# The first branch's projection in pairs of time blocks, and the end of a hybrid RWKV-7 / S5 block in two passes over weights kept in SBUF

## The chip, the core and the metric

The kernel runs on one core of one Trainium2 chip. The metric is the time of one execution on the device in microseconds (us), lower is better. TensorE is called PE here, its weight loads PEld, VectorE DVE, ScalarE ACT, GpSimd POOL, and SyncE, which only issues transfers, SP.

## The reference

One block of a streaming encoder over 2048 frames (T) of width 1024 (D), all in float32. An RMSNorm is followed by one input projection, whose columns feed two branches and three kinds of gates. The RWKV-7 branch has 16 heads of 64, the S5 branch 32 groups of 16 channels (width 512). Both are recurrences in time.

```python
h = rms_norm(x, norm_g)
zs, gate_a, u, gate_b, m_a, m_b = jnp.split(h @ w_in, SPLIT_POINTS, axis=-1)
...
y_a = y.reshape(bsz, seq, RWKV_WIDTH) * jax.nn.silu(gate_a)     # y: the RWKV-7 recurrence over zs
ys = jax.nn.gelu(s5_scan(u, ...))                               # 512 channels
g1, g2 = jnp.split(ys @ w_glu + b_glu, 2, axis=-1)
y_b = g1 * jax.nn.sigmoid(g2) * jax.nn.silu(gate_b)
merged = jax.nn.sigmoid(m_a) * (y_a @ p_a) + jax.nn.sigmoid(m_b) * (y_b @ p_b)
out = rms_norm(x + merged @ w_out, final_g)
```

w_in is 1024 x 7296, w_glu 512 x 1024, p_a and w_out 1024 x 1024, p_b 512 x 1024.

## The kernel before

**Products.** An f32 operand is split in a high part that PE takes as f32r (a copy on ACT) and the rest (a subtraction on DVE); helpers split and split_w do this. Each product is then three matmuls for every 128 rows of the contraction: high by high, high by low, low by high. Time is cut in four blocks (NTB) of 512 columns (TB). A product of 128 output channels by 512 columns is collected in one PSUM bank; over 1024 rows it has 24 matmuls, over 512 rows 12. A piece of weights is 512 x 128 (256 KB), held as 128 partitions x 512.

**The stream of jobs.** A Job (L471) is one column block of 128 weights of a large projection with one or two time blocks: it loads the weights in two pieces, splits them, and runs 24 matmuls for each time block, in steps of 6. `stream` (L519) runs the jobs one after another as a generator, and the sequential parts of the program (the RWKV scan, later the S5 loop) call it for a step whenever they have credit. So the order on PE is set by the program: a chain of small dependent matmuls, and between its links steps of 6 matmuls of jobs. A job whose `need` is not true yet makes `stream` yield without a matmul. `late` and `rest_` hold instructions that are put a step later on their engine. DVE is used through a wrapper (Woven, L75), so most of DVE's rows bear line 75, and the tiles tell them apart.

**The scan.** `scan` (L939) goes over units of a head pair and a time block, the last ones (7,2) and (7,3). In each chunk of 64 frames PE computes px, DVE copies it to rh, PE computes pu, DVE and ACT write SU, PE computes pn, and DVE writes the next chunk's SU. The branch's output y_a goes to DRAM (ya_d).

**The first branch's projection.** `stage_a` (L650) makes a job for one column block m of p_a and one time block (tiles raw_pa, whi_pa, wlo_pa, bank ppa); its end multiplies the gate sg and stores the product to pa_d. There are 32 such jobs, time block 0 first, m from 0 to 7 in each, so each weight is loaded and split four times. Their input comes from `load_ya` (L629), a background of other jobs that is called at each step of theirs: eight times it loads 128 rows into one of two tiles (tag xh) and splits the piece before it, in 19 steps in all, into yhi and ylo, of which there are two sets. The load of block 0 runs behind the last jobs of the projection before (pmb), that of block 1 behind the jobs of block 0, and so on. A job needs the whole block and all units of the scan before its own columns to be stored.

**The S5 loop.** `s5_run` (L1209) prepares tables (tables_e makes cw with DVE and ACT; `spread` copies cw to both halves of ce by two DMAs on SP, L1260; tables_m makes kps, mps and tps on PE) and then goes over 32 groups: head (px = input times a table on PE), middle (DVE: xx from px and ce, a running sum pp, yy), tail (py on PE), and a gelu for every second group. The steps of jobs that are left are spread over its 160 steps by a rate, (LEFT - KEEP) / 160, where LEFT is the number of steps left in the stream.

**The end** (L1609 to L1690) is outside of the section that is ordered by hand; there the scheduler of the tile framework orders the instructions by their dependences. For each time block: load ys and split it; for m in 0 to 3 load and split a weight of g2, 12 matmuls into one of two banks (pg), tanh on ACT, one DVE operation with gate_b (g2th), the same for g1, and split the result (ybhi, yblo); then for m in 0 to 7 load and split a weight of p_b, 12 matmuls (ppb), DVE operations with the gate (sgb) and the first branch's product (pal), and split the sum (mhi, mlo); then for four rows of 128 frames two products of 24 matmuls with w_out (pout, two banks of their own), the residual, the norm and a store on SP's queue. w_out is loaded and split once, in time block 0, and kept (wohi, wolo). The weights of the GLU and of p_b are loaded and split in each of the four time blocks.

## Time and profile before

| what | value |
|---|---|
| three runs | 2684.04 to 2690.86 us, median 2689.07 |
| the profiled execution's own time | 2685.18 us |
| its span in the trace | 2683.5 us |
| mean clock granted to PE | 0.991 of full speed |
| DRAM traffic | 220.43 MB read, 71.70 MB written |
| instructions | 48845 |

The profile is one execution. An engine's busy time says how long its instructions lasted, as the profiler has them; for PE the ends of matmuls are modelled, so the number of matmuls in a stretch is the better measure. Windows are given in us from the start of the span, and every window has the clock that PE was granted in it. A row of the timeline has start, length, engine, line, operation, tiles, and in brackets the idle time before it with what ended it. Where rows belong to groups, they have busy time and mean duration in ns, and then the idle time before. Buffer numbers are left out of names there.

The stretches of this execution that the change touches: the jobs of p_a begin in the last units of the scan, shortly after 1956 us; the first px of the S5 loop stands at 2125; the first product of the GLU begins at 2288; the last matmul ends at 2676.

### The profile page before, as it was taken

Reading aid. Unit: us, or ns where it says so; the run is one execution under the profiler, and the core shown is the slowest. Engines: PE = TensorE matmul, PEld = TensorE weight load, DVE = VectorE, ACT = ScalarE, POOL = GpSimd, SP = SyncE. Lnnn points to the kernel's source line nnn. Section 1 sums busy time; section 2 is a strip of 40 time slices with the busy share of each in tenths; the row PEclk is TensorE's granted clock in tenths of the full one; section 3 lists DMA queues with packets and bytes.
Section 4 is the critical chain, followed back from the end, with each engine's and each line's share of the span. In section 5 each row is a group of like instructions: output and inputs, shape, how many; then the busy total and the mean of one; then the engine's idle time right before and its main releaser. Section 6 shows DMA issues by size and latency. Waiting matters only on the chain. (4 is left out here: it accounts for less than half of the span.)

```text
span 2683.5 us, 48845 instructions
## 1 busy us (share of the span) xinstructions
PE 2594.4 (97%) x17164; PEld 1970.1 (73%) x17164; DVE 1865.4 (70%) x5572; ACT 1397.7 (52%) x3501; POOL 571.9 (21%) x955
## 2 busy tenths in 40 slices
PE   7999999999999999999999999999989899899998
PEld 5777777777777767777777777777767678677787
DVE  6656677776667778767776677776768798645644
ACT  5456555655555677555555555555644443423321
POOL 2221212122122333221212122121322201111110
PEclk9999999999999999999999999999999999999999
DMA  4232323233233543332323333232565755845532
GB/s 129 77 84 67 104 74 100 76 86 87 79 97 84 146 121 104 91 86 72 97 72 93 90 85 88 73 99 73 148 180 177 216 156 161 259 155 172 170 108 95
DMA packets 256491, 304.04 MB, mean 113 GB/s; under 512 B 159761, under 2 KB 172150, under 8 KB 255222
## 3 DMA queue, kind: packets, MB, share of 16 engines
q1 hardware_dynamic: 210646, 151.46, 21.0%
q0 software_dynamic: 45600, 149.46, 18.6%
q8 instruction: 135, 2.21, 0.3%
q14 instruction: 110, 0.90, 0.1%
HBM read 220.43 MB, written 71.70 MB: 109 GB/s over the span
## 5 line engine op out<-in xcount | busy, mean ns | idle before, releaser
L962 ACT ACTIVATE SU<-pu,dd 64x64 f32<-64x64 f32 x256 | 79.3, 310 | 350.5 <-DVE SU L75 286.5
L886 DVE TENSOR_TENSOR TM<-RF,IX 128x60 f32<-128x60 f32 (+24 forms) x992 | 207.2, 209 | 29.5 <-DMA IX<-ld 7.5
L890 DVE TENSOR_TENSOR RF<-RF,TM 128x60 f32<-128x60 f32 (+24 forms) x992 | 206.8, 208 | 27.4
L953 ACT ACTIVATE us<-SU,dec 64x64 f32<-64x64 f32 x512 | 176.4, 345 | 50.1 <-DVE SU L974 43.2
L75 DVE TENSOR_SCALAR SU<-pu,dd 64x64 f32<-64x64 f32 x256 | 69.8, 273 | 137.7 <-PE pu L960 60.7
L75 DVE TENSOR_TENSOR AT<-A,amask 64x256 f32<-64x256 f32 (+1 forms) x256 | 102.2, 419 | 63.1 <-PE A L835 41.9
L974 DVE SCALAR_TENSOR_TENSOR SU<-pn,dec,us 64x64 f32<-64x64 f32 x240 | 65.6, 273 | 115.1 <-PE pn L966 113.9
L840 ACT ACTIVATE AT<-A,dd 64x64 f32<-64x64 f32 x512 | 116.9, 303 | 48.2 <-PE A L835 43.1
L966 PEld LDWEIGHTS pn<-SU,BT 128*64 128x64 f32 x1024 | 56.3, 135 | 103.7 <-issue 39.4
L957 PEld LDWEIGHTS po<-AR,SU 64*64 64x64 f32 x1024 | 50.0, 131 | 97.3 <-issue 82.8
L75 DVE COPY rh<-px 128x128 f32<-128x128 f32 x256 | 74.0, 289 | 61.8 <-PE px L948 57.2
L948 PEld LDWEIGHTS px<-SU,AT 128*128 128x128 f32 x512 | 95.1, 189 | 29.7 <-DVE SU L75 9.0
L501 PE MATMUL ppa<-yhi,whi_pa 128*128 128x512 f32 x256 | 115.3, 450 | 0.3 <-DVE sg L75 0.3
L501 PE MATMUL pmb<-hhi,whi_mb 128*128 128x512 f32 x256 | 111.7, 436 | 0.0
L501 PE MATMUL pma<-hhi,whi_ma 128*128 128x512 f32 x256 | 111.1, 434 | 0.0
L501 PE MATMUL pga<-hhi,whi_ga 128*128 128x512 f32 x256 | 110.9, 433 | 0.0
L501 PE MATMUL pr<-hhi,whi_r 128*128 128x512 f32 x256 | 110.8, 433 | 0.0
L501 PE MATMUL pk<-hhi,whi_k 128*128 128x512 f32 x256 | 110.3, 431 | 0.0
L501 PE MATMUL pv<-hhi,whi_v 128*128 128x512 f32 x256 | 109.8, 429 | 0.3 <-ACT carry L454 0.3
L503 PE MATMUL ppa<-yhi,wlo_pa 128*128 128x512 f32 x256 | 103.8, 406 | 3.6 <-DVE wlo_pa L75 3.6
L948 PE MATMUL px<-SU,AT 128*128 128x128 f32 x512 | 100.0, 277 | 4.5 <-DVE SU L75 4.3
L502 PE MATMUL ppa<-ylo,whi_pa 128*128 128x512 f32 x256 | 103.5, 404 | 0.4 <-DVE ylo L75 0.4
(376 smaller groups left out, 7926.7 us busy)
## 6 DMA issues: line engine op xcount, KB each, us to landing
IX<-ld SPq DMA_DIRECT2D x128, 128.0 KB
raw_pa<-in_p_a_dram POOLq DMA_DIRECT2D x64, 256.0 KB, 4.3
raw_mb<-in_w_in_dram POOLq DMA_DIRECT2D x50, 256.0 KB, 3.6
raw_r<-in_w_in_dram POOLq DMA_DIRECT2D x36, 256.0 KB, 4.0
raw_k<-in_w_in_dram POOLq DMA_DIRECT2D x36, 256.0 KB, 3.9
raw_v<-in_w_in_dram POOLq DMA_DIRECT2D x36, 256.0 KB, 3.4
raw_ga<-in_w_in_dram POOLq DMA_DIRECT2D x34, 256.0 KB, 3.5
ce<-cw SPq DMA_DIRECT2D x16, 514.0 KB
```

The costliest lines, as they stand in the source:

```text
L75: r = f(*a, **kw)
L501: pe.matmul(ps, hi[:, k, :], xhi[:, kk_, :], start=(kk_ == 0), stop=False)
L502: pe.matmul(ps, hi[:, k, :], xlo[:, kk_, :], start=False, stop=False)
L503: pe.matmul(ps, lo[:, k, :], xhi[:, kk_, :], start=False, stop=(kk_ == 7))
L840: act.activation(out=at[HS[h], c, 0, h, :], in_=pas[h][HS[h], i, 0:C], func=AF.Copy, scale=dd[HS[h], c:c + 1])
L886: raw_dve.tensor_tensor(out=tm[:, 0:na, 0:nt], in0=rf[:, 0:na, s:s + 1].to_broadcast([P, na, nt]), in1=ix[:, s:s + 1, s + 1:32].to_broadca ...
L890: raw_dve.tensor_tensor(out=rf[:, 0:na, s + 1:32], in0=rf[:, 0:na, s + 1:32], in1=tm[:, 0:na, 0:nt], op=ALU.add)
L948: pe.matmul(px[:, 0:P], at[:, c, 0].rearrange("p h t -> p (h t)"), cur, start=True, stop=True)
L953: act.activation(out=us[HS[h]], in_=cur[HS[h], HS[h]], func=AF.Copy, scale=dec[HS[h]])
L962: act.activation(out=cur[64:128, 64:128], in_=pu[64:128, 0:C], func=AF.Copy, scale=dd[64:128, c:c + 1])
L966: pe.matmul(pn[HS[h], 0:C], bt[:, c, h, :], cur[:, HS[h]], start=True, stop=True)
L974: (raw_dve if h == 0 else dve).scalar_tensor_tensor(out=nxt, in0=pn[HS[h], 0:C], scalar=dec[HS[h]], in1=us[HS[h]], op0=ALU.mult, op1=ALU.add)
```

## The change

**The first branch's projection.** The column blocks 0 to 2 keep one job for each time block, the blocks 3 to 7 get jobs of two time blocks, (0, 1) and (2, 3), so that one weight tile serves 1024 columns. The order is now: 0 to 2 of block 0, 3 to 7 of blocks 0 and 1, 0 to 2 of block 1, 0 to 2 of block 2, 3 to 7 of blocks 2 and 3, 0 to 2 of block 3. So 44 pieces of p_a are loaded and split instead of 64. `load_ya` loads its eight pieces straight into ylo, four at a step, and splits them there in place: 11 steps instead of 19. The gate tiles come from one pool, and KEEP goes from 1 to 4. The loads of ys for the first time block wait until at most 12 steps of jobs are left.

**The end** is now ordered by hand and has two passes. Pass 1 does the GLU of all four time blocks, in 32 products of 12 matmuls that go round five PSUM banks, and stores y_b to DRAM (yb_d). With each product one piece of weights is fetched and one split: the last four of the GLU, eight of p_b and sixteen halves of w_out, and all stay in SBUF. Pass 2 goes over the four time blocks with p_b, the merge, w_out and the norm; y_b comes back from DRAM into yblo and is split in place. What closes a product is recorded behind the next product. The stores of the output go to POOL's queue, but for the last.

Loads of GLU weights go from 32 to 8, of p_b's from 32 to 8, of w_out from 8 of 512 KB to 16 of 256 KB, of gate_b from 4 of 1 MB to 16 of 256 KB; 16 stores and 16 loads of y_b come new. PE has 12750 instructions before and after, DVE 5574 and 5514, ACT 3439 and 3379.

The diff, cut:

```diff
-KEEP = 1
-SG0 = 4
-SG1 = 24
+KEEP = 4
-ALT = 2
...
+    yb_d = [dtile(f"yb_d{i}", [512, TB]) for i in range(NTB)]
...
-            raws = []
-            for k in range(9):
-                while k < 8 and (k, tb) not in YA:
+            for k in range(8):
+                while (k, tb) not in YA:
                     yield
-                if k < 8:
-                    raws.append(gp.tile([P, TB], F32, tag="xh", name=f"yraw{tb}_{k}"))
-                    pool.dma_start(out=raws[k], in_=ya_d[tb][k * P:(k + 1) * P, :])
+                pool.dma_start(out=hlo[:, k, :].bitcast(F32), in_=ya_d[tb][k * P:(k + 1) * P, :])
+                if k % 4 == 3:
                     yield
-                if k == 8:
-                    yield
-                    yield
-                    yield
-                if k:
-                    split_later(hhi[:, k - 1, :], hlo[:, k - 1, :], raws[k - 1])
-                    yield
+            yield
+            for k in range(8):
+                hi, lo = hhi[:, k, :], hlo[:, k, :]
+                act.copy(hi, lo.bitcast(F32))
+                rest_.append(lambda hi=hi, lo=lo: dve.tensor_tensor(out=lo, in0=lo.bitcast(F32), in1=hi.bitcast(F32), op=ALU.subtract))
+                yield
             YL.add(tb)
...
-                    pl, tag = (hp, "xw") if m % 2 and SG0 <= 8 * tb + m < SG1 else (gp, "sq")
+                    pl, tag = gp, "sq"
...
-            j.pre, j.alt, j.early = pre, 8 * tbs[0] + m >= ALT, SG0 <= 8 * tbs[0] + m < SG1
+            j.pre, j.alt, j.early = pre, (m, tbs) not in ((0, (0,)), (1, (0,))), False
...
-                    if j >= YJ and step in (0, 4):
+                    if j >= YJ and LEFT[0] <= 4 * len(one_) and step in (0, 4):
...
-        jobs += with_bg([stage_a(m, (0,)) for m in range(8)], load_ya(1), 1, False)
-        late_jobs = [stage_a(m, (1,)) for m in range(8)]
-        jobs += with_bg(late_jobs, load_ya(2), 1, False)
-        jobs += with_bg([stage_a(m, (2,)) for m in range(8)], load_ya(3), 1, False)
-        jobs += [stage_a(m, (3,)) for m in range(8)]
+        one_, two_ = range(3), range(3, 8)
+        jobs += with_bg([stage_a(m, (0,)) for m in one_], load_ya(1), 1, False)
+        jobs += [stage_a(m, (0, 1)) for m in two_]
+        jobs += with_bg([stage_a(m, (1,)) for m in one_], load_ya(2), 1, False)
+        jobs += with_bg([stage_a(m, (2,)) for m in one_], load_ya(3), 1, False)
+        jobs += [stage_a(m, (2, 3)) for m in two_]
+        jobs += [stage_a(m, (3,)) for m in one_]
...
+            banks = [psg, psg, psm, psm, psm]
+            turn_ = [0]
+
+            def bank(name):
+                pl = banks[turn_[0] % 5]
+                turn_[0] += 1
+                return pl.tile([P, TB], F32, tag="g" if pl is psg else "m", name=name)
...
+            def fetch():
+                w = next(wl, None)
+                if w:
+                    ST["n"] = ST.get("n", -1) + 1
+                    flying.append((load_4(w[0], w[1], (e0, wp)[ST["n"] % 2], "raw"), w[2]))
+
+            def split_next():
+                if flying:
+                    raw, dst = flying.pop(0)
+                    split_later(*dst, raw)
...
+            def close_glu(tb, m, h, ps):
+                if h == 2:
+                    th = ST["th", m] = e0.tile([P, TB], F32, tag="gth", name=f"g2th{m}_{tb}")
+                    act.activation(out=th, in_=ps, func=AF.Tanh, bias=col(57 + 4, m, pd), scale=0.5)
+                    dve.scalar_tensor_tensor(out=th, in0=th, scalar=1.0, in1=ST.pop(("gb", tb, m)), op0=ALU.add, op1=ALU.mult)
+                else:
+                    th = ST.pop(("th", m))
+                    dve.scalar_tensor_tensor(out=th, in0=ps, scalar=col(85, m), in1=th, op0=ALU.add, op1=ALU.mult)
+                    sp.dma_start(out=yb_d[tb][m * P:(m + 1) * P, :], in_=th)
+
+            def yb_load(tb):
+                YB[tb] = [wo.tile([P, 4, TB], F32R, tag="yb" + t_, name=f"yb{t_}{tb}") for t_ in ("hi", "lo")]
+                for k in range(4):
+                    sp.dma_start(out=YB[tb][1][:, k, :].bitcast(F32), in_=yb_d[tb][k * P:(k + 1) * P, :])
+
+            def yb_split(tb, k):
+                hi, lo = (t_[:, k, :] for t_ in YB[tb])
+                halves(hi, lo, lo.bitcast(F32), 0.25)
...
+            for m, h in first[:3]:
+                parts.append(bank(f"pg{h}{m}_0"))
+                product(parts[-1], WG[m, h], YS[0], range(3), 3)
             drain(ys0)
+            settle()
...
+            for tb in range(NTB):
+                bg = load_ys_apart(tb + 1) if tb + 1 < NTB else iter(())
+                for m in range(4):
+                    for h in (2, 1):
+                        settle()
+                        if parts:
+                            ps = parts.pop(0)
+                            product(ps, WG[m, h], YS[0], (3,), 3)
+                        else:
+                            ps = bank(f"pg{h}{m}_{tb}")
+                            product(ps, WG[m, h], YS[tb], range(4), 3)
+                        for f in pend:
+                            f()
+                        pend = [lambda tb=tb, m=m, h=h, ps=ps: close_glu(tb, m, h, ps)]
+                        split_next()
...
+                        fetch()
+                        if h == 1:
+                            mm = 4 * tb + m + 2
+                            if mm < 4 * NTB:
+                                load_gb(*divmod(mm, 4))
+                        next(bg, None)
+                        if n == 10:
+                            yb_load(0)
+                        if n in (20, 22, 24, 26):
+                            yb_split(0, (n - 20) // 2)
+                        n += 1
...
+                mh = [ep.tile([P, 8, TB], F32R, tag="m" + t_, bufs=1, name=f"m{t_}{tb}") for t_ in ("hi", "lo")]
+                for m in range(8):
+                    settle()
+                    ps = bank(f"ppb{m}_{tb}")
+                    product(ps, PB[m], YB[tb], range(4), 3)
+                    for f in pend:
+                        f()
+                    pend = [lambda m=m, ps=ps, tb=tb, mh=mh: close_b(tb, m, ps, mh)]
+                    if 2 <= m < 6:
+                        load_sg(tb, m + 2)
+                    if m == 6:
+                        load_xt(tb, 0)
+                for j in range(TB // P):
+                    for q in range(2):
+                        settle()
+                        ps = bank(f"pout{tb}_{j}_{q}")
+                        out_part(ps, mh, j, q, range(6 if j + q == 0 else 8))
+                        for f in pend:
+                            f()
+                        pend = []
+                        if j + q == 0:
+                            settle()
+                            out_part(ps, mh, j, q, range(6, 8))
+                        pend = [lambda tb=tb, j=j, q=q, ps=ps: close_out(tb, j, q, ps)]
+                        i = 2 * j + q
+                        if q and j + 1 < TB // P:
+                            load_xt(tb, j + 1)
+                        if tb + 1 < NTB:
+                            if i == 0:
+                                yb_load(tb + 1)
+                            if i in (1, 2):
+                                load_sg(tb + 1, 2 * i - 2)
+                                load_sg(tb + 1, 2 * i - 1)
+                            if 3 <= i < 7:
+                                yb_split(tb + 1, i - 3)
...
```

PE at the start of the scan's unit (7,2): pmb is the last product of the input projection, px, po, pu, pn and A belong to the scan, and ppa0 is the first product with p_a. Before:

```order
L503 MATMUL pmb73_3_23018<-hhi3_11426,wlo_mb73_1_22974 128x512
L948 MATMUL px_7_2_0_23126<-SU_7_2_22556,AT_7_2_22394 128x128
L957 MATMUL po_7_2_23125<-AR_7_2_22258,SU_7_2_22556 64x64 x2
L960 MATMUL pu_7_2_0_23136<-rh_7_2_0_23128,R64_7_2_22883 64x64 x2
L835 MATMUL A_7_3_0_0_23147<-AR_7_3_22994,BK_7_3_22942 128x128
L835 MATMUL A_7_3_0_1_23148<-AR_7_3_22994,BK_7_3_22942 128x128
L835 MATMUL A_7_3_0_0_23147<-AR_7_3_22994,BK_7_3_22942 128x128
```

After:

```order
L501 MATMUL pmb73_3_23024<-hhi3_11430,wlo_mb73_1_22980 128x512
L943 MATMUL px_7_2_0_23130<-SU_7_2_22560,AT_7_2_22398 128x128
L499 MATMUL ppa0_0_4_23137<-yhi0_22826,whi_pa0_0_0_23040 128x512
L500 MATMUL ppa0_0_4_23137<-ylo0_22827,whi_pa0_0_0_23040 128x512
L501 MATMUL ppa0_0_4_23137<-yhi0_22826,wlo_pa0_0_0_23041 128x512
```

The first job of p_a stood behind the whole unit (7,2), between whose links only rows of the next unit (A) were; now its matmuls follow the unit's first px.

PE at the start of the S5 loop: px and py are head and tail of a group, kps, mps and tps the tables of the next four groups, ppa6_2 and ppa3_2 products with p_a for time block 2. Before:

```order
L1328 MATMUL px0_25174<-uR_0_24790,m1_0_24975 128x256
L1329 MATMUL px0_25174<-uR_0_24790,m2_0_24976 128x256
L1328 MATMUL px1_25183<-uR_0_24790,m1_0_24975 128x256
L1329 MATMUL px1_25183<-uR_0_24790,m2_0_24976 128x256
L501 MATMUL ppa6_2_6_25202<-yhi2_24030,whi_pa6_2_0_25146 128x512
L502 MATMUL ppa6_2_6_25202<-ylo2_24031,whi_pa6_2_0_25146 128x512
L503 MATMUL ppa6_2_6_25202<-yhi2_24030,wlo_pa6_2_0_25147 128x512
```

After, from the tables that follow px2 and the first py on:

```order
L1288 MATMUL kps_1_24997<-s5_cst1_24526,i1_1_24967 128x16 x4
L1291 MATMUL mps_1_25002<-ident_105,i1_1_24967 128x128 x4
L1323 MATMUL px3_25027<-uR_0_24685,m1_0_24866 128x256
L1324 MATMUL px3_25027<-uR_0_24685,m2_0_24867 128x256
L1352 MATMUL py0_24993<-uR_0_24685,tk_0_24948 128x256
L1353 MATMUL py0_24993<-yy1_25009,o1_0_24924 128x256
L1354 MATMUL py0_24993<-yy1_25009,o2_0_24925 128x256
L1307 MATMUL tps_1_25041<-ks_1_25016,sel_24675 128x64 x8
L1323 MATMUL px4_25065<-uR_1_24965,m1_1_25011 128x256
L1324 MATMUL px4_25065<-uR_1_24965,m2_1_25012 128x256
L499 MATMUL ppa3_2_6_25075<-yhi2_24409,whi_pa3_2_0_24862 128x512
```

Before, a job's matmuls stood behind px1, and again behind mps; after, the steps from px0 to px4 follow each other with no job between them.

DVE in p_b's products of time block 1: sgb<-sgb,ppb closes a product, sgb<-sgb,pal adds the first branch, mlo is the split of the sum. Before:

```order
L75 SCALAR_TENSOR_TENSOR sgb0_1_27418<-sgb0_1_27418,ppb0_1_27405 128x512
L75 TENSOR_TENSOR wlo_pb3_1_27483<-raw_pb3_1_27480,whi_pb3_1_27482 128x512
L75 TENSOR_TENSOR sgb0_1_27418<-sgb0_1_27418,pal0_1_27420 128x512
L75 SCALAR_TENSOR_TENSOR sgb1_1_27445<-sgb1_1_27445,ppb1_1_27432 128x512
L75 TENSOR_TENSOR wlo_pb4_1_27510<-raw_pb4_1_27507,whi_pb4_1_27509 128x512
L75 SCALAR_TENSOR_TENSOR mlo1_27398<-sgb0_1_27418,mhi1_27397 128x512
L75 TENSOR_TENSOR sgb1_1_27445<-sgb1_1_27445,pal1_1_27447 128x512
L75 TENSOR_TENSOR yslo2_27872<-ysraw2_2_27881,yshi2_27871 128x512
```

After:

```order
L72 SCALAR_TENSOR_TENSOR sgb0_1_27353<-sgb0_1_27353,ppb0_1_27569 128x512
L72 TENSOR_TENSOR sgb0_1_27353<-sgb0_1_27353,pal0_1_27355 128x512
L72 SCALAR_TENSOR_TENSOR mlo1_27568<-sgb0_1_27353,mhi1_27567 128x512
L72 SCALAR_TENSOR_TENSOR sgb1_1_27357<-sgb1_1_27357,ppb1_1_27590 128x512
L72 TENSOR_TENSOR sgb1_1_27357<-sgb1_1_27357,pal1_1_27359 128x512
L72 SCALAR_TENSOR_TENSOR mlo1_27568<-sgb1_1_27357,mhi1_27567 128x512
```

The splits of p_b's weights (wlo_pb) and of the next block's ys (yslo) stood between the closings; now the closings stand alone.

More of the change, by code (lines that the diff above doesn't have):

```diff
@@ new lines, in ys_load, with ys_split @@
+        def ys_load(tb, k):
+            if k == 3 and tb == 0:
+                return YR3[0]
+            pl, tag = (e0, "ysr") if tb else (gp, "xh")
+            raw = pl.tile([P, TB], F32, tag=tag, bufs=2, name=f"ysraw{tb}_{k}")
+            sp.dma_start(out=raw.rearrange("p (s c) -> p s c", s=SC), in_=ys_d[k][:, :, tb * 64:(tb + 1) * 64])
+            return raw
+        def ys_split(tb, k, raw):
+            if tb not in YS:
+                pl, tag, nk = (e0, "ys", 4) if tb else (hp, "h", 8)
+                YS[tb] = [pl.tile([P, nk, TB], F32R, tag=tag + t_, bufs=2, name=f"ys{t_}{tb}") for t_ in ("hi", "lo")]
+            hi, lo = (t_[:, k, :].rearrange("p (c s) -> p c s", s=SC) for t_ in YS[tb])
+            split_later(hi, lo, raw.rearrange("p (s c) -> p c s", s=SC))
@@ new lines, in tile_rwkv7_s5_block, with product @@
+            banks = [psg, psg, psm, psm, psm]
[4 more added lines that the diff above has]
+                return pl.tile([P, TB], F32, tag="g" if pl is psg else "m", name=name)
+            def product(ps, w, xs, ks, last):
+                (hi, lo), (xhi, xlo) = w, xs
+                for k in ks:
+                    pe.matmul(ps, hi[:, k, :], xhi[:, k, :], start=(k == 0), stop=False)
+                    pe.matmul(ps, hi[:, k, :], xlo[:, k, :], start=False, stop=False)
+                    pe.matmul(ps, lo[:, k, :], xhi[:, k, :], start=False, stop=(k == last))
@@ new lines, in close_b, with out_part @@
+                halves(mh[0][:, m, :], mh[1][:, m, :], sg, 0.5)
+            def out_part(ps, mh, j, q, ks):
+                js, qs = slice(j * P, (j + 1) * P), slice(q * 512, (q + 1) * 512)
+                (mhi, mlo), (whi, wlo) = mh, ST["wo"]
+                for k in ks:
+                    pe.matmul(ps, mhi[:, k, js], whi[:, k, qs], start=(k == 0), stop=False)
+                    pe.matmul(ps, mhi[:, k, js], wlo[:, k, qs], start=False, stop=False)
+                    pe.matmul(ps, mlo[:, k, js], whi[:, k, qs], start=False, stop=(k == 7))
@@ L1691 @@
+            settle()
+            for f in pend:
+                f()
+            settle()
 _INS = ['x', 'norm_g', 'w_in', 'mu_shift', 'w0', 'w_up', 'a0', 'a_up', 'k_k', 'k_a', 'r_k', 'lnx_g', 'lnx_b',
```

213 lines of the change are left out of this document (118 added, 95 removed).

## The prediction

> **What bounds the kernel now.** I read the page's first part, then the tail of the span in windows of 50 us, then the waits of that tail, and last the stretch from 1900 to 2300 us in finer windows and in order of time. The page says that TensorE (PE) is never long idle:
>
> ```profile
> span 2683.5 us, 48845 instructions
> PE 2594.4 (97%) x17164; PEld 1970.1 (73%) x17164; DVE 1865.4 (70%) x5572; ACT 1397.7 (52%) x3501; POOL 571.9 (21%) x955
> ```
>
> The change issues the same matmuls in another order, so PE's own work stays and only its lost time can move. Busy time hides losses, since ends of matmuls are modelled; their number does not. In the final product, 192 matmuls in a row (timeline of PE, first and last):
>
> ```profile
> 2632.26 0.39 PE L1676 MATMUL pout<-wohi,mhi 128*128 128x512 f32 x1
> ...
> 2675.55 0.39 PE L1678 MATMUL pout<-wohi,mlo 128*128 128x512 f32 x1
> ```
>
> 43.29 us over 191 steps is 0.2266 us each, so a full window of 50 us holds 220.6. The end's windows (columns: stretch, length, PE, PEld, DVE, ACT, POOL busy with their counts, granted clock, DMA share, GB/s) hold:
>
> ```profile
> 2290.00:2300.00 10.00, 8.40 (x34) 5.98 (x33) 6.44 (x9) 2.35 (x3) 1.49 (x2) 1.00 0.56 153
> ...
> 2300.00:2350.00 50.00, 41.85 (x168) 30.68 (x168) 34.34 (x47) 25.17 (x35) 9.74 (x13) 1.00 0.93 289
> 2350.00:2400.00 50.00, 48.03 (x206) 38.09 (x207) 22.27 (x37) 10.72 (x24) 3.92 (x6) 1.00 0.45 151
> 2400.00:2450.00 50.00, 46.42 (x199) 36.67 (x198) 36.90 (x56) 22.96 (x36) 11.88 (x16) 1.00 0.71 201
> 2450.00:2500.00 50.00, 48.78 (x214) 39.73 (x214) 19.10 (x35) 9.53 (x22) 4.08 (x7) 1.00 0.34 113
> 2500.00:2550.00 50.00, 44.42 (x188) 34.15 (x187) 34.51 (x52) 21.25 (x32) 10.90 (x15) 1.00 0.67 193
> 2550.00:2600.00 50.00, 50.00 (x222) 41.36 (x222) 18.35 (x34) 10.72 (x24) 4.49 (x7) 1.00 0.33 110
> 2600.00:2650.00 50.00, 49.56 (x217) 40.02 (x216) 30.26 (x47) 14.45 (x25) 5.06 (x7) 1.00 0.36 107
> ```
>
> From 2300 on that is 1414 matmuls where 7 x 220.6 = 1544 fit: 130 x 0.2266 = 29.5 us lost, at full clock, most in the windows where DVE is busy; the 10 us before lose 1.6 in idle time. The waits of 2288 to 2684 name the cause:
>
> ```profile
> ACT whi_glu L252 <- PE pg L241: 22.2, 14, 3.6
> DVE sgb L75 <- DMA sgb<-sb_d: 15.8, 14, 2.8
> PE ppb L240 <- DVE sgb L75: 10.8, 12, 1.9
> ```
>
> Weights of the GLU and of p_b are loaded and split anew in every time block. ACT waits for a buffer that PE still reads, DVE waits for a late load, and PE waits until DVE has emptied one of two PSUM banks.
>
> **Part 1, the end in two passes.** All splits of weights in pass 2 are gone, those of pass 1 come one per product. A product of 12 matmuls takes 12 x 0.2266 = 2.72 us. A time block of pass 1 (21.8 us) costs DVE 8 splits of weights, 4 of ys and 8 GLU operations. By these rows (window 2288 to 2684)
>
> ```profile
> L75 DVE TENSOR_TENSOR wlo_glu<-raw_glu,whi_glu 128x512 fp32r<-128x512 f32 x31 | 21.2, 687 | 10.7 <-ACT whi_glu L252 9.4 <-PE pg L242 1.3
> L75 DVE TENSOR_TENSOR yslo<-ysraw,yshi 128x512 fp32r<-128x512 f32 x14 | 14.9, 1077 | 3.7 <-ACT yshi L252 3.6
> L75 DVE SCALAR_TENSOR_TENSOR g2th<-pg,prm,g2th 128x512 f32<-128x512 f32 x16 | 12.0, 748 | 9.4 <-PE pg L242 9.4
> ```
>
> that is at most 5.5 + 4.3 + 6.0 = 15.8 us, under PE's 21.8. In pass 2 DVE does three operations a product, each much like this one, 2.1 us under 2.72:
>
> ```profile
> L75 DVE SCALAR_TENSOR_TENSOR mlo<-sgb,mhi 128x512 fp32r<-128x512 f32 x32 | 22.1, 689 | 9.4 <-ACT mhi L255 8.9
> ```
>
>  Five PSUM banks, and loads issued two or three products (5.4 to 8.2 us) early, leave PE nothing late in steady running. Lost will be the start of pass 1 (one load into freed memory before the fourth weight) and some late pieces: 5 us, between 1 and 12. Gain 29.5 - 5 = 24.5, between 17.5 and 28.5. The closing steps behind the last matmul stay.
>
> The Trainium skill, "TensorE: Matmul & The Clock Gate", section "Wait — 56ns, not 53.3ns?", gives 215.7 ns from start to start for 512 columns at full clock. By that the end's 1536 matmuls would take 16.7 us less than at 226.6 ns, and as much more would be to gain. The row decides: this stretch was dense and at clock 1.00, and the change alters no matmul.
>
> **Part 2, the first branch's projection.** Four things happen between 1936 and 2290 us. First, a hole in the scan. The window before it and the hole's own, and the hole's two longest idle gaps:
>
> ```profile
> 1916.00:1936.00 20.00, 19.11 (x177) 14.36 (x172) 17.17 (x42) 12.01 (x25) 9.20 (x14) 1.00 0.56 155
> 1936.00:1956.00 20.00, 14.21 (x103) 10.05 (x101) 10.02 (x29) 15.59 (x46) 3.13 (x9) 0.74 0.44 124
> ...
> 1938.80 0.33 PE L957 MATMUL po<-AR,SU 64*64 64x64 f32 x4 [1.96 <-ACT y L756]
> ...
> 1955.76 0.71 PE L966 MATMUL pn<-SU,BT 128*64 128x64 f32 x3 [2.72 <-DVE SU L75]
> ```
>
> Here ppa may not begin, since its input (19 steps of loading and splitting) is not ready; the scan's chain runs bare, and the clock falls to 0.74. Idle 5.8 plus 0.26 x 14.2 of lost clock: 9.5 us. After, all 8 loads are issued at once and ppa follows pmb without a gap. The window before shows what stays, 0.9: gain 8.6, between 4 (splits of the next block now fall here) and 9.5.
>
> Second, to fourth, the rest of the scan, the S5 start and the S5 loop:
>
> ```profile
> 1956.00:2093.00 137.00, 127.94 (x735) 92.36 (x733) 110.21 (x422) 54.68 (x125) 41.19 (x64) 0.96 0.67 193
> 2093.00:2138.00 45.00, 39.91 (x182) 32.37 (x182) 28.18 (x52) 19.84 (x49) 12.42 (x17) 0.95 0.84 239
> 2138.00:2288.00 150.00, 142.28 (x695) 119.88 (x694) 132.69 (x241) 63.09 (x131) 14.23 (x19) 0.96 0.57 156
> L75 DVE TENSOR_TENSOR wlo_pa<-raw_pa,whi_pa 128x512 fp32r<-128x512 f32 x64 | 43.8, 684 | 9.8 <-ACT whi_pa L224 9.5
> ```
>
> Lost in the scan: 9.1 idle + 0.04 x 127.9 clock = 14.2 us. By the order of instructions, DVE has here 34 splits and closings of ppa instead of 58: 24 x 0.684 = 16.4 us of its 110 less. PE waits there for the chain through DVE, so I take half, 7 us, between 0 and 14.
>
> The S5 start gets worse. The pairs need block 3 of the input, whose last column comes from the last scan unit, and only three jobs (72 matmuls) are left to cover it, where eight were. So PE has no ppa from the first px to the fifth. What then sets the pace is DVE and the loads, seen in order of time in the kernel before (DVE, SP's issues, ACT, PE):
>
> ```profile
> 2115.12 1.29 DVE L75 TENSOR_TENSOR cw<-cw,cwt 128x512 f32<-128x512 f32 x2 [0.99 <-ACT cw L1244]
> 2126.55 0.69 DVE L75 TENSOR_TENSOR ylo<-yraw,yhi 128x512 fp32r<-128x512 f32 x1 [4.61 <-ACT yhi L224]
> 2128.36 0.68 DVE L75 TENSOR_TENSOR xx<-px,ce 128x512 f32<-128x512 f32 x1
> 2132.33 0.68 DVE L75 TENSOR_TENSOR yy<-pp,ce 128x512 f32<-128x512 f32 x1
> 2137.84 0.23 DVE L75 TENSOR_TENSOR cwt<-cw,s_e 128x64 f32<-128x64 f32 x1 [4.83 <-ACT cw L1227]
> 2116.49 1.15 SPq L1260 DMA_DIRECT2D ce<-cw  x2
> 2128.83 1.12 SPq L1260 DMA_DIRECT2D ce<-cw  x2
> 2137.39 0.41 ACT L1227 COPY cw<-s_e 128x36 f32<-128x36 f32 x2 [9.26 <-issue]
> 2119.05 1.89 PE L1312 MATMUL tps<-ks,sel 128*128 128x64 f32 x16
> 2125.03 0.59 PE L1328 MATMUL px<-uR,m 128*128 128x256 f32 x2
> 2125.47 0.59 PE L1329 MATMUL px<-uR,m 128*128 128x256 f32 x2
> ```
>
> The bare stretch starts when the third job ends, about 2106 on this clock. cw ends 2 us earlier than 2116.4, as ppa's splits before it are gone; the spread then lands about 8.5 us later (issue 2128.83 to ACT's 2137.39), at 2123; yy follows after 4.6 us (2128.36 to 2133.0). The second spread is queued right behind the first and lands between 2123 and 2131; three steps of the chain more, some 7 us, and ppa resumes between 2135 and 2139. PE's own work in these 29 to 33 us is two tps (1.9 each) and some 16 px and py of 0.44 with kps and mps, about 11 us. Idle is 18 to 22, and 2 more for the half clock behind it. The window 2093 to 2138 loses 5.1 + 0.05 x 39.9 = 7.1 now. Net loss 14 us, between 5 (the spreads land in 4 us, as raw_glu does below) and 27.
>
> The loop loses 7.7 + 0.04 x 142.3 = 13.4 us now. It has about four splits less and the chain has a lead; I take 4, between 0 and 9.
>
> Sum: 24.5 + 8.6 + 7 - 14 + 4 = 30.1, and the 1.6 of 2290 to 2300, where half-ready GLU products wait now and dense ppa stands after: 32 us. The profiled execution took 2685.18 us with a span of 2683.5; it becomes 2653. It lies 3.9 under the median of the runs, 2689.07, against which the forecast is 2689 - 32 = **2657 us**.
>
> **The rivals.** (a) Transfers bound pass 1; slower than before. It moves 28 pieces of weights, 12 ys, 16 gb, 16 yb out, 4 yb in, each 256 KB, and 0.5 MB more: 20.4 MB in 87 us, 234 GB/s.
>
> ```profile
> 2420.00:2430.00 10.00, 9.20 (x40) 7.10 (x39) 7.74 (x12) 6.79 (x9) 2.25 (x3) 1.00 0.98 255
> raw_glu<-in_w_glu_dram POOLq DMA_DIRECT2D x32, 256.0 KB, 4.5
> ```
>
> This window, with ys in it, was full at 255 GB/s, and 2300:2350 gave 289. Loads lie 5 to 8 us ahead, over raw_glu's 4.5 to landing. It decides once pass 1 takes over 119 us, below 171 GB/s; at 160 it takes 127, and the time is 2697. Against: those two rows. Chance 0.07. (b) The bare stretch lasts twice as long, 65 us, because the last column's store and load (DVE waited 4.61 us for it, and now nothing covers) come one after the other with the spreads: 32 more lost, 2689, no change. Chance 0.09. (c) The scan and loop lose almost nothing, as DVE was their bound, and the bare stretch costs 5: 24.5 + 9 + 13 + 9 - 5 + 2 = 52, 2637. Chance 0.13. (d) A rule of its own: going round PSUM banks makes the clock swing. Short gaps did take it to 0.74 in 1936:1956; at 0.74 the end's 348 us become 470, and the time 2779. The end ran at 1.00 with two banks and waits up to 1.9 us. Chance 0.02. The Trainium skill tells this in "TensorE: Matmul & The Clock Gate", "A second HAM failure mode: psum-queue depth-cycling"; no run here shows it yet.
>
> **How the numbers follow.** The forecast has 0.69, its own bounds 2640 to 2676. About 0.3%, 8 us, can be told from no change. Faster: 0.69 + 0.13 = 0.82. Same: (b), 0.09. Slower: (a) and (d), 0.09. The range reaches to most of (c) and to the edge of (b): 2636 to 2680.
>
> **What would show it.** Right: the windows of the last 350 us hold 215 to 221 matmuls of 50 us each; ppa begins without a gap and the clock stays at 1.00 there; between the first px and the next ppa PE idles some 20 us and the clock falls. Wrong: 50 us windows of pass 1 under 200 matmuls with a DMA share near 1; a bare stretch beyond 45 us or under 20; an unchanged wait of PE for SU in the last scan unit.

## The result and the profile after

The changed kernel takes 2667.91 us (median of 4 runs, 2666.92 to 2672.18); the kernel before took 2689.97 beside it. The ratio is 0.9928, with an interval of 0.9913 to 0.9942: 16 to 23 us of 2690 are gained, where 32 were forecast. In the three later series, in which the experiments ran, the kernel before took 2683.4 to 2685.2 us; against those, a comparison across series, the gain is 15.5 to 17.3. The profiled execution is the slowest of the four, 2672.18 us with a span of 2670.3. The page's first part:

```profile
span 2670.3 us, 48574 instructions
PE 2585.2 (97%) x17164; PEld 1969.7 (74%) x17164; DVE 1824.8 (68%) x5512; ACT 1356.0 (51%) x3441; POOL 536.5 (20%) x918
```

PE stays the bound with the same matmuls; 13.2 us of span are gone. Windows of the end (columns as in the prediction: stretch, length, then PE, PEld, DVE, ACT, POOL busy with counts, clock, DMA share, GB/s):

```profile
2300.00:2350.00 50.00, 48.44 (x208) 38.58 (x206) 28.66 (x40) 21.99 (x32) 12.73 (x19) 1.00 0.85 262
2350.00:2400.00 50.00, 49.46 (x217) 40.73 (x218) 27.83 (x41) 19.19 (x30) 4.85 (x9) 1.00 0.58 178
2400.00:2450.00 50.00, 48.54 (x208) 38.45 (x207) 23.35 (x38) 9.86 (x21) 2.33 (x4) 1.00 0.55 187
2450.00:2500.00 50.00, 50.00 (x216) 40.24 (x215) 25.66 (x43) 9.58 (x20) 3.39 (x6) 1.00 0.42 148
2500.00:2550.00 50.00, 50.00 (x216) 40.23 (x215) 24.63 (x42) 10.22 (x22) 3.39 (x6) 1.00 0.35 116
2550.00:2600.00 50.00, 50.00 (x216) 40.20 (x215) 17.95 (x34) 9.14 (x22) 3.95 (x7) 1.00 0.37 126
2600.00:2650.00 50.00, 50.00 (x216) 40.22 (x215) 22.52 (x37) 7.95 (x16) 2.83 (x5) 1.00 0.36 116
```

The 188 and 168 matmuls of the windows before are gone, and the second half holds 216 in every window. But it is dense (PE busy 50.00 of 50.00) and holds 216, not the 222 of before's densest window (2550 to 2600): from start to start a matmul takes 0.2333 us there instead of 0.2266. (A window also counts a matmul that only reaches over its edge, so 222 and not 220.6 is what 0.2266 gives.) Pass 1 moves up to 262 GB/s and isn't held up; the clock is 1.00.

The place of the old hole, and PE's order there:

```profile
1936.00:1956.00 20.00, 19.44 (x139) 14.55 (x138) 11.73 (x27) 17.15 (x49) 9.28 (x19) 1.00 0.79 258
```

```profile
1936.35 0.38 PE L943 MATMUL px<-SU,AT 128*128 128x128 f32 x2
1936.49 0.47 PE L499 MATMUL ppa<-yhi,whi_pa 128*128 128x512 f32 x1
```

ppa follows without a gap, at clock 1.00 instead of 0.74. The start of the S5 loop, in windows, and all that PE waited for from 2093 to 2145 us:

```profile
2102.00:2112.00 10.00, 0.00 (x0) 0.00 (x0) 7.73 (x13) 7.10 (x15) 2.03 (x3) 0.60 0.56 159
2112.00:2122.00 10.00, 1.22 (x2) 0.50 (x2) 4.41 (x8) 1.03 (x2) 0.00 (x0) 0.50 1.01 199
2122.00:2132.00 10.00, 8.69 (x30) 7.55 (x31) 9.10 (x22) 3.09 (x8) 0.00 (x0) 0.53 0.13 35
```

```profile
PE py L1352 <- ACT tk L1313: 11.0, 1, 11.0
PE py L1353 <- DVE yy L72: 9.4, 1, 9.4
```

20.4 us idle, and matmuls at half clock behind it, from 2123 on: the bare stretch that was forecast. In order of time, what stood ahead of it (DVE, SP's issues):

```profile
2100.36 0.69 DVE L72 SCALAR_TENSOR_TENSOR sg<-sg,ppa 128x512 f32<-128x512 f32 x1 [3.11 <-DMA sg<-sa_d]
...
2105.82 1.29 DVE L72 TENSOR_TENSOR cw<-cw,cwt 128x512 f32<-128x512 f32 x2 [2.04 <-ACT cw L1239]
...
2118.62 0.69 DVE L72 TENSOR_TENSOR xx<-px,ce 128x512 f32<-128x512 f32 x1 [4.87 <-DMA ce<-cw]
...
2107.18 5.77 SPq L1255 DMA_DIRECT2D ce<-cw  x4
```

cw is ready at 2107.1 and its spread lands 11.4 us after the first issue, where 8.5 were taken. DVE had stood 3.1 us for a gate tile, with cw's steps queued behind it.

**By stages.** The starts of six matmuls in each timeline cut the stretch from the last product of the input projection to the first of the GLU: last pmb, last pn (end of the scan), first px, 17th px, last px, first pg. (In the kernel before, 8 matmuls of pg run between the last ones of ppa, and the last ppa stands for the first pg.) A dense run of ppa gives the price of the filling matmuls:

```profile
2290.19 0.40 PE L500 MATMUL ppa<-ylo,whi_pa 128*128 128x512 f32 x1
...
2300.93 0.39 PE L501 MATMUL ppa<-yhi,wlo_pa 128*128 128x512 f32 x1
```

10.74 us over 46 steps are 0.2335. The table has the length of each stage less 0.2335 for each matmul of ppa (and, in the kernel before, of pg) in it, so that stages with different filling compare. "Total" is what isn't filling; the last column is the whole length of the end, from there to the start of the last pout. All are in us. The kernels below the second row are experiments; those with a pad under all the large tiles are left out, since their filling has another price.

| kernel | scan | to first px | px 1 to 17 | loop | rest | total | end |
|---|---|---|---|---|---|---|---|
| before | 53.5 | 12.1 | 16.1 | 92.0 | 5.6 | 179.3 | 379.2, and 8 pg done |
| after | 42.9 | 13.4 | 34.5 | 87.1 | 7.8 | 185.7 | 361.4 |
| pa_only | 42.2 | 13.4 | 37.0 | 84.7 | 8.9 | 186.2 | 378.8 |
| end_only | 52.8 | 11.3 | 16.0 | 93.6 | 6.1 | 179.8 | 364.5 |
| end_ya | 44.6 | 16.7 | 19.6 | 95.8 | 6.3 | 183.0 | 366.4 |
| ya_old | 62.4 | 19.8 | 32.5 | 85.0 | 4.9 | 204.6 | 362.8 |
| one5b | 42.4 | 17.0 | 24.7 | 93.3 | 8.7 | 186.1 | 365.3 |
| one8b | 52.9 | 18.6 | 20.5 | 91.7 | 7.8 | 191.5 | 359.8 |
| one8 | 42.8 | 17.3 | 20.9 | 89.6 | 7.3 | 177.9 | 362.5 |
| two_banks | 39.7 | 15.2 | 34.1 | 84.8 | 7.4 | 181.2 | 365.6 |
| after_wo_al | 41.7 | 14.6 | 35.3 | 85.3 | 7.3 | 184.2 | 356.6 |

From before to after: scan 10.6 less, to the first px 1.3 more, start of the loop 18.4 more, loop 4.9 less, rest 2.2 more: together 6.4 us more. The end: 379.2 and 8 x 0.2335 of work already done make 381.1; 361.4 is 19.7 less. 19.7 - 6.4 = 13.3, the 13.2 of span. Four rows (after, pa_only, two_banks, after_wo_al) have the same code in these stages and total 181.2 to 186.2, so a single trace tells some 5 us in the sum, and the scan or the start of the loop to about 3. The end has the same code in seven rows (after, end_only, end_ya, ya_old, one5b, one8b, one8) and takes 359.8 to 366.4, so there a difference of less than 7 us between single traces tells nothing.

### The profile page after: what moved, and what is told of

The parts are those of the page before. It is cut to its first block, busy times and chain, and to the rows that moved or that the text cites. A ratio compares the mean times of both kernels' runs of the same rounds, so it can differ in the third digit from the quotient of the medians.

```text
span 2670.3 us, 48574 instructions
## 1 busy us (share of the span) xinstructions
PE 2585.2 (97%) x17164; PEld 1969.7 (74%) x17164; DVE 1824.8 (68%) x5512; ACT 1356.0 (51%) x3441; POOL 536.5 (20%) x918
## 3 DMA queue, kind: packets, MB, share of 16 engines
q1 hardware_dynamic: 212134, 147.80, 20.4%
## 4 chain that ended last, share of the span: by engine, by line
PE 46%; DVE 6%; DMA 5%; issue 2%; ACT 2%; SPq 1%; POOL 0%; DVEq 0%; POOLq 0%; ACTq 0%
PE pout L1787 2%; PE pout L1786 2%; PE pout L1788 2%; PE ppa L499 1%; PE pma L499 1%; PE A L830 1%; PE pn L961 1%; PE ppa L500 1%; PE ppa L501 1%; DMA ce<-cw 1%; PE pma L500 1%; PE po L952 1%; PE pma L501 1%; PE pga L499 1%; PE pr L499 1%
## 5 line engine op out<-in xcount | busy, mean ns | idle before, releaser
L961 PE MATMUL pn<-SU,BT 128*64 128x64 f32 x1024 | 94.5, 246 | 12.1 <-DVE SU L72 10.1
```

Source lines behind the costliest of these rows:

```text
L961: pe.matmul(pn[HS[h], 0:C], bt[:, c, h, :], cur[:, HS[h]], start=True, stop=True)
```

## The experiments

Theory A: the matmuls of pass 2 are slower because of the addresses of their operands. Rival B: because of the PSUM banks or pools. The next three kernels decide it. They change nothing but addresses.

**One pad of 32 bytes.** In the program as built, the right-hand stack of SBUF ends at byte 229344 of a partition, 32 past a multiple of 64, and so all its large tiles start there. w_out lay on the left before (150208, a remainder of 64 by 128, like mhi's 113344); after the change it lies on the right (143328, remainder 96; mhi 88704, remainder 0).

```diff
+    rpad = ctx.enter_context(tc.tile_pool(name="rpad", bufs=1, side="right"))
+    rpad.tile([P, 8], F32, tag="rpad", name="rpad")
     phr = ctx.enter_context(ExitStack())
```

> The changed kernel with a tile of 32 bytes at the far end of the right-hand stack of SBUF, so that every tile there starts 32 bytes lower, at a multiple of 64 bytes. No instruction changes but its addresses. Theory A: a matmul of 512 columns whose moving operand starts 32 bytes past a multiple of 64 takes 0.2333 us from start to start, one that starts on a multiple takes 0.2266. 7680 matmuls change sides: 7680 x 0.0067 = 51 us less, some of it lost where PE waits for the scan: 2618 us, between 2612 and 2640, and 220 matmuls in 50 us in the second pass instead of 216. Rival B: the pitch of 0.2333 comes from five PSUM banks or from the place of the weights, and addresses do nothing: 2668 us and 216 matmuls as before.

Measured: 2654.69 us (before beside it 2685.24), ratio 0.9883, 0.9867 to 0.9899, against 0.9928 unpadded: faster, by a quarter of what was expected. Pass 2 holds 220 matmuls in 50 us:

```profile
2500.00:2550.00 50.00, 50.00 (x220) 41.03 (x219) 25.00 (x43) 10.45 (x22) 2.82 (x5) 1.00 0.44 154
```

B falls, also by the kernel two_banks below, whose pass 2 takes 269.9 us with two banks against 270.6 with five. A's numbers are wrong: the pitch, the time from one start to the next, went to 0.2289 there and not to 0.2266. Most of what the pad gains lies ahead of the changed stretches, where the jobs of the input projection run. The start of their last matmul, after and here (in the unpadded kernels it lies between 1932.7 and 1939.8):

```profile
1936.12 0.39 PE L501 MATMUL pmb<-hhi,wlo_mb 128*128 128x512 f32 x1
```

```profile
1926.33 0.39 PE L503 MATMUL pmb<-hhi,wlo_mb 128*128 128x512 f32 x1
```

Of the 17.5 us between these two executions 9.8 are gained up to there, and 3.2 in pass 2. So most of the pad's gain has nothing to do with the change; whether it would speed up the kernel before as well was not tried.

**The pad only ahead of w_out and y_b.**

```diff
+                            rp = ph3.enter_context(tc.tile_pool(name="rp", bufs=1, side="right"))
+                            rp.tile([P, 8], F32, tag="rp", name="rp")
                             wo = ph3.enter_context(tc.tile_pool(name="wo", bufs=1, side="right"))
```

> The changed kernel with 32 bytes ahead of the pool that holds w_out and y_b, so that only the 1152 matmuls of pass 2 read moving operands that start on a multiple of 64 bytes. Theory A: 1152 x 0.0067 = 7.7 us less, 2660 us, between 2657 and 2663, with 220 matmuls in 50 us in pass 2. Rival B: no change, 2668 us.

Measured: 2666.61 us, ratio 0.9934 (0.9920 to 0.9947): by time not told from the changed kernel, where 7.7 us were expected. The trace tells it. First ppb and last pout of pass 2, after and here:

```profile
2391.97 0.40 PE L1644 MATMUL ppb<-ybhi,pb0hi 128*128 128x512 f32 x1
...
2662.55 0.39 PE L1788 MATMUL pout<-wohi,mlo 128*128 128x512 f32 x1
```

```profile
2388.43 0.40 PE L1644 MATMUL ppb<-ybhi,pb0hi 128*128 128x512 f32 x1
...
2655.89 0.39 PE L1790 MATMUL pout<-wohi,mlo 128*128 128x512 f32 x1
```

270.6 and 267.5 us, 3.1 less (267.4 with the pad under all tiles). In the seven other kernels with the new end and no pad the same stretch took 269.8 to 270.5, so 3 us are well told.

**A pad of 96 bytes** in place of 32, after which the moving operands and weights of the large products all start on multiples of 128.

```diff
-    rpad.tile([P, 8], F32, tag="rpad", name="rpad")
+    rpad.tile([P, 24], F32, tag="rpad", name="rpad")
```

> The changed kernel with 96 instead of 32 bytes at the far end of the right-hand stack: all moving operands of the large products and all their weights then start on a multiple of 128 bytes. Theory A2, from the first two runs (pitch 0.2270 where moving operand and weights have the same remainder by 128, 0.2289 to 0.2300 where they differ by 64, 0.2335 where they differ by 32): all products go at 0.2270, 0.003 x 7680 = 23 us of PE less than with 32 bytes, of which the first run let one half through: 2643 us, between 2636 and 2650, and 220 matmuls in 50 us in the second pass. Rival: only the remainder by 64 counts, and the rest is something else: 2655 us and a pitch of 0.2300 as with 32 bytes.

Measured: 2653.63 us, ratio 0.9887 (0.9873 to 0.9900), the same as with 32 bytes and what the rival had for the time. The trace again, pass 2 and three of its windows:

```profile
2380.80 0.39 PE L1646 MATMUL ppb<-ybhi,pb0hi 128*128 128x512 f32 x1
...
2644.33 0.39 PE L1790 MATMUL pout<-wohi,mlo 128*128 128x512 f32 x1
```

```profile
2450.00:2500.00 50.00, 50.00 (x223) 41.40 (x222) 25.68 (x43) 9.36 (x20) 3.39 (x6) 1.00 0.50 167
2500.00:2550.00 50.00, 50.00 (x222) 41.44 (x221) 24.75 (x42) 10.45 (x22) 2.82 (x5) 1.00 0.45 160
2550.00:2600.00 50.00, 50.00 (x222) 41.40 (x221) 24.53 (x43) 10.22 (x22) 3.96 (x7) 1.00 0.36 121
```

263.5 us, 7.1 less than after: A2 holds in pass 2. That the difference of the two remainders counts, and not that of the moving operand alone, is shown by the kernel before: its w_out and mhi both have 64 and go at 0.2266, while 64 against 0 goes at 0.2289 (after_pad). In the stream of jobs A2 fails: the mean time from one job matmul to the next, over some 4500 pairs in each trace, is 0.2306 us, as with 32 bytes (0.2303; 0.2336 unpadded). Why equal remainders don't bring 0.2267 there stays open.

**The two parts apart.** The change of the first branch alone, with the old end; and the new end alone, with the old jobs.

```diff
+KEEP = 4
...
+        one_, two_ = range(3), range(3, 8)
+        jobs += with_bg([stage_a(m, (0,)) for m in one_], load_ya(1), 1, False)
+        jobs += [stage_a(m, (0, 1)) for m in two_]
...
```

> The kernel before with the change of the first branch's projection alone (pairs, new load of y_a, KEEP), and the old end. The prediction's terms 8.6 + 7 - 14 + 4 make 5.6 us less than before: 2684. Theory from the changed kernel's trace (9 us gained between the last product of the input projection and the first px, 14 lost from there to the last py): 5 us more than before, 2695. Rival (c) of the prediction, the scan and the loop gain and the bare stretch costs little: 17 us less or more, under 2673.

Measured: 2685.31 us (12 runs) against 2685.24, ratio 1.0001 (0.9992 to 1.0009). The first branch's change is worth nothing, between 2 us of gain and 2 of loss. Its profiled execution, the slowest of the twelve, has the stages of the changed kernel, 11 us gained in the scan and 21 lost at the S5 start.

```diff
-KEEP = 4
+KEEP = 1
...
-        jobs += with_bg([stage_a(m, (0,)) for m in one_], load_ya(1), 1, False)
+        jobs += with_bg([stage_a(m, (0,)) for m in range(8)], load_ya(1), 1, False)
...
```

> The changed kernel with the old order of the first branch's projection, the old load of y_a and KEEP 1; the end in two passes stays. The prediction's terms 24.5 + 1.6 make 26 us less than before: 2664. Theory A with the changed kernel's trace: waits fall by 23 us, but 1152 matmuls have a moving operand 32 bytes past a multiple of 64 and cost some 6 us more: 17 us less than before, 2673. If the end's waits are not what the change removes: within 5 us of before.

Measured: 2669.04 us, ratio 0.9938 (0.9925 to 0.9951): 16 us less than before, the 17 of theory A. As far as the runs tell, the end brings the whole gain.

**The load of y_a.** The changed kernel with the old load, and the new end with the old jobs and the new load.

```diff
-                pool.dma_start(out=hlo[:, k, :].bitcast(F32), in_=ya_d[tb][k * P:(k + 1) * P, :])
...
+                    raws.append(gp.tile([P, TB], F32, tag="xh", name=f"yraw{tb}_{k}"))
+                    pool.dma_start(out=raws[k], in_=ya_d[tb][k * P:(k + 1) * P, :])
...
```

> The changed kernel with the old load of y_a (two tiles, a load and a split in turn, 19 steps) and all else as changed, pairs too. Step of the prediction: the old load leaves the hole of 1936 to 1956, 8.6 us: 2677 us, and the clock falls there. Theory G with H (the pairs, not the load, are what the scan gains by): the hole returns, but the splits come spread out, and the sum is within 4 us of 2668. If the 12 steps of three single jobs don't hold 19 steps of loading, PE stands still longer before blocks 2: over 2680.

Measured: 2693.21 us, ratio 1.0037 (1.0023 to 1.0052), 25 us slower in the medians than with the new load. The hole and what follows it:

```profile
1936.00:1956.00 20.00, 14.99 (x106) 10.78 (x107) 10.12 (x34) 14.67 (x43) 4.04 (x10) 0.71 0.44 126
1956.00:1976.00 20.00, 18.31 (x80) 13.96 (x79) 9.79 (x27) 6.40 (x12) 8.56 (x13) 0.95 0.69 199
```

The hole is back, and the scan stage has 62.4 instead of 42.9: three single jobs have 12 steps, and 19 steps of loading don't fit. With only three single jobs ahead of them, pairs can't be had with the old load.

> The kernel with the new end and the old order of jobs (2669 us), and with the new load of y_a alone: eight loads in two steps, splits in place. Step of the prediction: the hole closes, 8.6 us less, 2660 us. Theory H (eight splits in a row stand before the scan's own work on DVE and ACT, the more so where every job brings splits of its own): the hole closes and as much or more is lost behind it, 2669 to 2680 us.

(Its diff is the one above, turned round, on end_only.) Measured: 2669.51 us, ratio 0.9949 (0.9934 to 0.9964), no gain against end_only's 2669.04. The first window and the largest wait of PE from the end of the scan to the first px:

```profile
1936.00:1956.00 20.00, 19.71 (x143) 14.85 (x144) 10.75 (x26) 16.11 (x46) 8.60 (x19) 1.00 0.84 271
```

```profile
PE ppa L503 <- DVE ylo L75: 5.4, 5, 2.0
```

The hole is closed, with single jobs too: the scan stage has 44.6 instead of 52.8, so 8.2 us less, close to the 8.6 of the prediction. Then it is given back: 5.4 us to the first px, as PE now waits for splits of ylo that come in a row at the end of the load, 3.6 at the S5 start, 2.2 in the loop. Theory H had the sum right.

**Filling the bare stretch.** Theory C says more single jobs would cover it; D that their splits cost as much.

```diff
-        one_, two_ = range(3), range(3, 8)
+        one_, two_ = range(5), range(5, 8)
```

> The changed kernel with five single jobs for each time block instead of three, and pairs for column blocks 5 to 7 only: 8 more pieces of p_a are loaded and split. Theory C (pairs keep two input blocks in use, so only the single jobs can cover the load of the next block): the 120 matmuls of five jobs last 28 us instead of 16.8, the wait for ylo of block 2 (3 us and 2 of half clock) goes and the bare stretch at the start of the S5 loop is up to 11 us shorter: 2656 us, between 2652 and 2661. Rival D: DVE sets the pace here, and 8 x 0.69 us of splits more cost what the cover gains: 2668 us or a little more.

Measured: 2677.83 us, ratio 0.9975 (0.9965 to 0.9986): 10 us or more slower than after. C falls. The stage from px 1 to 17 did shrink by 9.8 us, but 3.6 more went ahead of it and 6.2 more in the loop. These sum to nothing, and the 10 us of the runs are not to be seen in this trace: its execution was the third fastest of eight, that of the changed kernel the slowest of four, and they lie 2.9 us apart. Where the 10 us go stays open.

```diff
-        one_, two_ = range(3), range(3, 8)
+        one_, two_ = range(8), range(8, 8)
```

> The changed kernel without any pairs: eight single jobs for each time block as before the change, 64 pieces of p_a; the new load of y_a and the new end stay. Theory C: the hole of 1936 to 1956 stays closed (10 us against the kernel with the old load) and the bare stretch is gone: 2669 - 10 = 2659 us, between 2655 and 2663. Rival D: the 20 splits more (13.7 us of DVE) are what the pairs were worth: 2672 us or more.

Measured: 2679.69 us, ratio 0.9982 (0.9973 to 0.9990). C falls again: the hole is closed, but the scan stage is back at 52.9. It differs from end_ya (44.6) in KEEP, in when the loads of ys may begin, and in that gate tiles of the middle jobs aren't loaded early; in its scan PE waited 5.5 us for rh and 4.7 in one piece for SU, both behind DVE. The rows tell what DVE stood for (SP's issue, DVE, PE):

```profile
2002.21 0.43 SPq L652 DMA_DIRECT2D sg<-sa_d  x1
...
2006.28 0.69 DVE L72 SCALAR_TENSOR_TENSOR sg<-sg,ppa 128x512 f32<-128x512 f32 x1 [5.43 <-issue]
2006.88 0.28 DVE L72 COPY rh<-px 128x128 f32<-128x128 f32 x1
...
2007.22 0.48 PE L955 MATMUL pu<-rh,R 64*64 64x64 f32 x4 [4.67 <-DVE rh L72]
```

The gate tile of the sixth product is fetched late, DVE stands 5.4 us before that product's closing, and the scan's rh is queued behind it. In end_ya, which loads this gate early, the sixth closing starts at 1995.94 with no idle time ahead of it.

```diff
-                    if j >= YJ and LEFT[0] <= 4 * len(one_) and step in (0, 4):
+                    if j >= YJ and LEFT[0] <= 4 * len(one2_) and step in (0, 4):
...
-        jobs += with_bg([stage_a(m, (2,)) for m in one_], load_ya(3), 1, False)
-        jobs += [stage_a(m, (2, 3)) for m in two_]
-        jobs += [stage_a(m, (3,)) for m in one_]
+        one2_ = range(8)
+        jobs += with_bg([stage_a(m, (2,)) for m in one2_], load_ya(3), 1, False)
+        jobs += [stage_a(m, (2, 3)) for m in range(8, 8)]
+        jobs += [stage_a(m, (3,)) for m in one2_]
```

Blocks 2 and 3 get eight single jobs each; blocks 0 and 1 keep their pairs.

> The changed kernel with pairs only for time blocks 0 and 1; blocks 2 and 3 get eight single jobs each as before the change: 10 more pieces of p_a are loaded and split. Theory G, from the stages of ten traces (with pairs the two last units of the scan lose 11 us less; at the start of the S5 loop, which runs bare, 18 us more): the gain in the scan stays and the bare stretch goes, against some 5 us more lost in the loop: 12 us less than the changed kernel, 2656 us, between 2652 and 2660, and 7 to 12 us lost between px0 and px16 instead of 25. Rival D (splits decide everywhere; the kernel without any pairs took 2680): 2668 to 2675 us.

Measured: 2668.72 us, ratio 0.9942 (0.9929 to 0.9955): not told from the changed kernel. In this trace G shows:

```profile
2093.00:2113.00 20.00, 17.71 (x80) 13.37 (x80) 9.33 (x16) 10.94 (x27) 3.92 (x5) 1.00 0.49 156
2113.00:2133.00 20.00, 12.93 (x54) 10.08 (x54) 13.34 (x23) 5.33 (x10) 5.02 (x7) 0.80 1.00 252
```

134 matmuls in 40 us with ppa between, 20.9 instead of 34.5 in the stage, the scan's gain kept; 3.9 and 2.5 us are lost again ahead of it and in the loop, and the total is 7.8 less. But this profiled execution took 3.1 us less than its kernel's median and that of the changed kernel 4.3 more, so the runs see none of the 7.8. G's mechanism, that single jobs fill the bare stretch, stands; its 12 us don't.

**Two PSUM banks in the end.**

```diff
-                pl = banks[turn_[0] % 5]
+                pl = banks[turn_[0] % 5] if turn_[0] < 3 else psg
```

> The changed kernel with two PSUM banks in turn for all products of the end, but for the first three. Theory E (the banks are what frees PE): of the 29.5 us lost before, the 12 waits of ppb for sgb had 10.8 and come back: 2678 us. Rival F (a bank is emptied late only because DVE is held by splits and late loads, and those are gone): up to 3 us more, 2668 to 2671 us.

Measured: 2673.74 us, ratio 0.9966 (0.9954 to 0.9979): some 6 us more than after by the medians, some 10 by the ratios. PE's waits in the end, here and after:

```profile
PE pg L1644 <- DVE g2th L72: 2.8, 3, 2.0
PE pg L1644 <- ACT g2th L1688: 1.7, 1, 1.7
PE pg L1644 <- issue: 1.5, 1, 1.5
PE ppb L1644 <- DVE sgb L72: 1.0, 1, 1.0
```

```profile
PE pout L1786 <- ACT mhi L1649: 1.5, 1, 1.5
PE pg L1645 <- DVE yslo L72: 1.2, 2, 0.6
PE pg L1644 <- ACT yshi L222: 0.9, 1, 0.9
```

ppb's wait for sgb, 10.8 us in the kernel before, comes back with 1.0: there the late splits and loads did it, as F says. Waits for a bank return in the GLU, 4.5 us, more than F's 3. The trace has 4 us more in the end, which lies within the 359.8 to 366.4 of the unchanged end. PE's waits there sum to 7.0 us against 3.6, and the runs lose 6 to 10: between E (10) and F (up to 3) this isn't settled.

**Both together**, one8 with the pad of 96 bytes:

> Pairs only for time blocks 0 and 1, and 96 bytes at the far end of the right-hand stack of SBUF, so that moving operands and weights of the end have the same remainder by 128. Theory G and the address rule: 2656 - 14 = 2642 us, between 2637 and 2648, the fastest of all. If the bare stretch is not what one8 removes: 2654 us as with the 96 bytes alone.

Measured: 2653.95 us, ratio 0.9889 (0.9873 to 0.9905). It beats both kernels, but by no more than the pad alone (2653.63).

## Why the prediction was right, and where its sizes were off

The time fell, by the end's waits, and lies inside the range; 32 us were forecast and 19 (0.72%) came. By the runs, the end gave 16 of its 26 us and the first branch none of its 5.6 (8.6 + 7 - 14 + 4). So the direction comes from the end alone, and that the time lies inside is owed to a range of over 20 us to each side.

- **The end, 24.5 and 1.6 forecast, 16 by the runs of end_only, 19.7 in the trace.** The mechanism held: splits and loads off the path, clock 1.00. PE's waits left are 3.6 us. The step that failed is "The row decides: ... the change alters no matmul". It altered their addresses: pass 2 takes 270.6 us, and 263.5 with the operands on equal remainders. These 7.1 us are all of what is missing by the trace (6.4) and most of it by the runs (10). The 0.2266 was a price of before's pout alone: the jobs of the same kernel go at 0.2336. The loss itself was sized a little low, since the windows count matmuls over their edges: by starts, 1405 matmuls begin from 2300 to 2650 before the change, and 31.5 us are lost there, not 29.5.
- **The hole, 8.6 forecast, 8.2 measured** (scan stage, end_only to end_ya): the load closes it, as forecast.
- **The rest of the scan, 7 forecast, about 2 measured.** Scan and hole together gained 10.6, which is told to about 3. The step was that PE waits for the chain through DVE, whose work falls. With all singles and early gates the new load alone gives 44.6 (end_ya), with pairs 42.9, so fewer splits are worth some 2; without early gates all singles have 52.9 (one8b), but there a wait of 4.7 us goes back to one more late gate tile. What the splits alone are worth isn't told closer than that. The prediction named an unchanged wait of PE for SU in the last unit as a sign of being wrong. In that unit, (7,3), PE waits for SU in neither kernel; its waits for SU stand in (7,2), and they did not shrink. Those of the scan stage, before and after:

```profile
PE px L948 <- DVE SU L75: 3.1, 2, 1.9
PE pn L966 <- DVE SU L75: 2.7, 1, 2.7
```

```profile
PE pn L961 <- DVE SU L72: 5.9, 1, 5.9
PE px L943 <- DVE SU L72: 1.7, 2, 1.3
```

That is 5.8 us before and 7.6 after. What the longest wait goes back to is no work of DVE's:

```profile
1963.70 0.69 DVE L72 SCALAR_TENSOR_TENSOR sg<-sg,ppa 128x512 f32<-128x512 f32 x1 [4.03 <-DMA sg<-sa_d]
...
1964.41 0.27 DVE L72 TENSOR_SCALAR SU<-pu,dd 64x64 f32<-64x64 f32 x1
...
1964.73 0.77 PE L961 MATMUL pn<-SU,BT 128*64 128x64 f32 x3 [5.91 <-DVE SU L72]
```

The scan's SU stands on DVE behind the closing of a ppa product, which waits for its gate tile. The kernel before has such a wait too (5.1 us, at 1968.96). Its early loads begin with the fifth job; loading the first gates earlier was not tried.
- **The S5 start, 14 lost forecast (5 to 27), 18.4 measured.** Idle was 20.4 us, within the 18 to 22. For the half clock behind it 2 us were taken; it lasted eight us of matmuls (2123 to 2131), which is a loss of some 4, an estimate from the clock of 0.50.
- **The loop, 4 forecast, 4.9 measured, and 2.2 lost behind it.** Neither these 2.2 us nor the 1.3 lost between the scan and the first px have a term of their own in the sum.
- **Rivals.** (a) falls: pass 1 takes 90.8 us, against 87. (b) falls: from the last ppa ahead of the first px to the next one, 2096.94 to 2134.10, are 37 us, not 65. (c) falls by the S5 start. (d) falls: with five banks in turn the clock is 1.00 in the windows of the whole end. (In other traces of this end it fell for a few us, as to 0.50 from 2343 to 2346 in end_only; in pa_only the old end with its two banks has the same, 0.51 from 2321 to 2324.) The swing that the Trainium skill tells of in "TensorE: Matmul & The Clock Gate", section "A second HAM failure mode: psum-queue depth-cycling", does not show here. The 215.7 ns that the Trainium skill gives in "TensorE: Matmul & The Clock Gate", section "Wait — 56ns, not 53.3ns?", is met by no kernel here: the best stretch has 0.2266 us.
